# In the first down unit of a round P4 stands between P6 and P7, with a bank of its own, and the next norm's operands are made two products later

## The chip, the cores and the metric

The kernel runs on one core of a Trainium2 chip. The metric is the device time of one execution in microseconds (us): the median of three runs of the kernel before is 1251.46 us (1251.28 to 1251.55).

## The reference, cut to what matters

The program is one inference step of a two-layer decoder for 576 tokens (512 of a prompt, 64 of samples) and a model width of 1024. Each layer is a mixer and then an MLP; the change touches only the MLP's second product and the operands of the norm that follows it.

```python
def sqrelu_mlp(h, w_up, w_down):
    return jnp.square(jax.nn.relu(h @ w_up)) @ w_down
...
hp = hp + sqrelu_mlp(rmsnorm(hp, norm_mlp[l]), mlp_w_up[l], mlp_w_down[l])
```

`w_up` is 1024 x 4096, `w_down` is 4096 x 1024, everything in float32.

## The kernel before

**Operands in two parts.** TensorE (PE) multiplies a rounded type, so each float32 operand is cut into a high and a low part, and every product is three sets of matmuls: high weight by high activation, high weight by low activation, low weight by high activation. For a weight block of 128x512, ScalarE (ACT) makes the high part (`whi`, line 248) and VectorE (DVE) the low part (`wlo`, line 259). Six buffers of each exist (`NW_`). The raw weights come by DMA in tiles of 512 KB (`raw`, line 218), three buffers, in the order in which they are used.

**Rounds.** The 4096 inner columns of an MLP are done in four rounds of 1024. A round has eight up products (48 matmuls each), whose results are made into activations, and then a down part that adds into the residual `h0` to `h7` (128 rows of the model width by 576 tokens each). The last round of the second layer is done in another way, so seven rounds have the down part that the change touches: four in the first MLP (P6 of their unit 0 starts at 317.14, 417.22, 516.00 and 617.33 us of the span) and three in the second (895.57, 994.33 and 1093.17 us).

**Down units.** The down part of a round is four units, `m` = 0 to 3; unit `m` adds to rows `h[2m]` and `h[2m+1]`. A unit is a 2x2 block product done with seven products instead of eight (Winograd's form of Strassen's scheme): P1 to P7, each of 12 matmuls of 128x288. The weights of P1, P2 and P4 are blocks a11, a12 and a22 of the unit's two raw tiles; those of P5, P6, P7 and P3 are sums s1 to s4 that DVE makes first (line 233): s1 = a21+a22, s2 from s1 and a11, s3 from a21 and a11, s4 from s2 and a12. `UNIT` is the order of the products in units 1 to 3 (P1, P5, P6, P2, P7, P3, P4), `FIRST_UNIT` the order in unit 0.

**Chains through the banks.** Intermediate sums stay in PSUM: P6 is added onto P1 in bank `x` (half of an `acc` tile), ACT copies that to a bank `z`, P7 is added onto it there, ACT copies that to `w`, P4 is added there. DVE takes each finished bank into `h` (`to_h`, line 511). The banks `y`, `f`, `g`, `z`, `w` are four buffers in turn. In unit 0 the P1, P2, P3 and P5 products go first (three of their four parts while the last activations are still being made), P1's result is kept in `v`, the other half of the same `acc` tile, and then come P6, P7 and P4. In units 1 to 3, `y` is a copy of P1's bank, made between P1 and P6 (line 546), `z` one of P6's (line 552), `w` one of P7's (line 557).

**What sets the order.** DVE and ACT run in the order in which the code issues to them (`manual_schedule`); TensorE's order is left to a scheduler. After each product `ahead_to` issues the casts, low parts and sums for the weights of later products (up to five ahead), so those stand in the DVE and ACT queues between the `to_h` operations and the copies.

**Between two reads of one PSUM tile** by different engines the build puts a wait: in unit 0 the copy `z<-x` (line 535) stands behind DVE's `h += v` (the third call on line 511 after `shared(f)`), since `v` and `x` are one tile.

**The next norm.** In the fourth round of the first MLP each finished residual row goes to `nxt.chunk`: ACT makes `xhi` (line 391) and a square (line 401), DVE `xlo` (line 392), GpSimd (POOL) adds the square to a sum (line 407). Those calls stand right after the unit that finished the rows. They are the operands of the next layer's projections.

Of the kernel before, what the change touches and what calls it, by code (L numbers as in the profile page):

```python
# [14 lines left out]
ALU = mybir.AluOpType  # L15
# [98 lines left out]
NCOL = 59  # L114
UNIT = ("P1", "P5", "P6", "P2", "P7", "P3", "P4")
SUMS = {"P1": "s1", "P5": "s2", "P2": "s3", "P6": "s4"}
FIRST_UNIT = ("P1", "P2", "P3", "P5", "P6", "P7", "P4")


@with_exitstack  # L120
def hybrid_step(ctx: ExitStack, tc: tile.TileContext, a, o):
    nc = tc.nc
# [27 lines left out]
    h, first = [], []  # L150
# [37 lines left out]
    def add_unit(pair, first):  # L188
        jobs.extend((n, len(order)) for n in (FIRST_UNIT if first else UNIT))
        order.extend(pair)  # L190
# [17 lines left out]
    used, done, summed = [0], [0], [0]  # L208
# [17 lines left out]
    def total(k, i):  # L226

        if (k, i) not in sums:
            b = blocks_of(i)
            x, y = {"s1": ("a21", "a22"), "s2": ("s1", "a11"), "s3": ("a21", "a11"), "s4": ("s2", "a12")}[k]  # L230
            x = b[x] if x in b else total(x, i)
            sums[k, i] = sum_pool[0].tile([P, 512], F32, name=k, tag="sum", bufs=4)
            nc.vector.tensor_tensor(out=sums[k, i], in0=x, in1=b[y], op=ALU.add)  # L233
        return sums[k, i]
# [37 lines left out]
    def ahead_to(n):  # L272

        n = min(n, len(jobs))
        while len(parts) < n or owed:
            while summed[0] < min(len(parts) + 2, len(jobs)):
                job, i = jobs[summed[0]]
                k = SUMS.get(job)
                if k:
                    total(k, i)  # L280
                summed[0] += 1
            if len(parts) < n:
                prepare()
            split_low()
        load_to(done[0] + 3)
# [144 lines left out]
    def rounds_of(norm, nxt, mp):  # L430
        rounds = 32 // FB
# [12 lines left out]
        for r in range(rounds):  # L444
            plain = nxt is None and r == rounds - 1
            acts = []
# [36 lines left out]
                acts.append((hi, lo))  # L483
            if plain:
                return [acts[2 * p + j] for j in range(2) for p in range(FB // 2)]
            for m in range(KC // 2):
                down_unit(acts, m, m == 0)
                if r == rounds - 1:
                    nxt.chunk(2 * m)
                    nxt.chunk(2 * m + 1)  # L490

    def down_unit(acts, m, first):


        operand = {"P1": 0, "P2": 2, "P3": 1, "P5": 3, "P6": 4, "P7": 5, "P4": 6}
        row1, row2 = h[2 * m], h[2 * m + 1]
        both = acc_tile()
        x, v = both[:, 0, 0:TH], both[:, 1, 0:TH]
        n2, n1 = slice(0, TH), slice(TH, T)

        def bank(name):
            return m_tile(name)[:, 0:TH]

        def run(n, out, start, stop=True, ks_=range(4), w=None, ahead=NW_ - 1):
            w = w or take(1)[0]
            product(out, w, lambda k: [t[:, operand[n]] for t in acts[k]], ks_, start, stop)
            if ahead:
                ahead_to(used[0] + ahead)

        def to_h(row, cols_, src, op):  # L510
            nc.vector.tensor_tensor(out=row[:, cols_], in0=row[:, cols_], in1=src, op=op)  # L511

        def shared(src):
            to_h(row1, n2, src, ALU.add)
            to_h(row2, n2, src, ALU.subtract)

        if first:

            y, g, f = bank("y"), bank("g"), bank("f")
            early = [("P1", x), ("P2", y), ("P3", g), ("P5", f)]  # L520
            ws = take(4)
            for (n, out), w in zip(early, ws):
                run(n, out, True, False, range(3), w, 0)
            for (n, out), w in zip(early, ws):
                run(n, out, False, True, [3], w, 0)
                if n == "P1":
                    nc.scalar.copy(out=v, in_=x)
            ahead_to(used[0] + 2)
            run("P6", x, False, ahead=2)
            to_h(row1, n1, y, ALU.add)  # L530
            to_h(row1, n2, g, ALU.add)
            shared(f)
            to_h(row1, n1, v, ALU.add)
            z = bank("z")
            nc.scalar.copy(out=z, in_=x)
            to_h(row1, n2, x, ALU.add)
            run("P7", z, False, ahead=3)
            w_ = bank("w")
            nc.scalar.copy(out=w_, in_=z)
            to_h(row2, n2, z, ALU.subtract)  # L540
            run("P4", w_, False, ahead=4)
            to_h(row2, n1, w_, ALU.subtract)
            return
        run("P1", x, True)
        y = bank("y")
        nc.scalar.copy(out=y, in_=x)  # L546
        f = bank("f")
        run("P5", f, True)
        shared(f)
        run("P6", x, False)  # L550
        z = bank("z")
        nc.scalar.copy(out=z, in_=x)
        run("P2", y, False)
        to_h(row1, n1, y, ALU.add)
        run("P7", z, False)
        w_ = bank("w")
        nc.scalar.copy(out=w_, in_=z)
        to_h(row2, n2, z, ALU.subtract)
        run("P3", x, False)
        to_h(row1, n2, x, ALU.add)  # L560
        run("P4", w_, False)
        to_h(row2, n1, w_, ALU.subtract)
# [774 lines left out]
```

## Time and profile before

| | |
|---|---|
| median of three runs | 1251.46 us |
| the profiled execution | 1251.84 us |
| its span, first to last instruction | 1249.8 us |
| mean granted TensorE clock | 0.991 |
| PE busy | 1207.0 us, 97% |
| DVE busy | 850.8 us, 68% |
| ACT busy | 585.7 us, 47% |
| POOL busy | 193.2 us, 15% |

A row of the timeline has the start, the duration, the engine, the line, the operation with output and inputs, and, in brackets, how long the engine had been idle and what ended that. "x4" merges four instructions in a row; PE instructions overlap, so what four matmuls cost is read from one start to the next. A row of a table of windows has the stretch, its length, the engine's busy time and number of instructions, the mean granted TensorE clock (1.00 is full), the DMA share and GB/s.

### The profile page before, as it was taken

The numbers are of one execution on the slowest core, as the hardware profiler recorded it, in microseconds if no ns is written. First come the engines' busy times: TensorE is split into PE (matmuls) and PEld (weight loads), VectorE is DVE, ScalarE is ACT, GpSimd is POOL, SyncE is SP. The second block draws the span as 40 slices with busy tenths as digits, with TensorE's granted clock in tenths as the row PEclk, the third lists the DMA queues.
The fourth block names the chain that finished last, engine by engine and source line by source line (L and its number), as shares of the span: only waits on it lengthen the run. The fifth ranks groups of instructions, "written<-read, shape, count | busy, mean of one in ns | idle before, by whom it ended". The sixth has DMA issues, their size and how long they took to land.

```text
span 1249.8 us, 22699 instructions
## 1 busy us (share of the span) xinstructions
PE 1207.0 (97%) x9213; PEld 1190.4 (95%) x9213; DVE 850.8 (68%) x1539; ACT 585.7 (47%) x1108; POOL 193.2 (15%) x166
## 2 busy tenths in 40 slices
PE   8999999999999999999999999999999999999996
PEld 8999999999999999999989988999999999999996
DVE  8877785456856866775796778546875784784455
ACT  5333554444434434443466777444443453443363
POOL 3543330110000000000023554220000000000223
PEclk9999999999999999899999999999999999999998
DMA  7244222222232242142224212122132233124253
GB/s 278 95 128 122 72 87 72 81 68 85 69 119 68 68 119 85 51 121 69 65 85 123 69 35 69 52 85 68 52 122 80 68 101 103 51 86 118 84 150 113
DMA packets 38521, 113.62 MB, mean 91 GB/s; under 512 B 4161, under 2 KB 11521, under 8 KB 38401
## 3 DMA queue, kind: packets, MB, share of 16 engines
q1 hardware_dynamic: 37408, 110.31, 29.0%
q8 instruction: 72, 1.18, 0.4%
q0 software_dynamic: 320, 1.31, 0.3%
q10 hardware_dynamic: 688, 0.55, 0.1%
q14 instruction: 33, 0.26, 0.1%
HBM read 107.12 MB, written 6.03 MB: 91 GB/s over the span
## 4 chain that ended last, share of the span: by engine, by line
PE 87%; DVE 6%; ACT 3%; issue 2%; DMA 1%; SPq 0%; DVEq 0%; POOL 0%; ACTq 0%
PE acc L304 54%; PE acc L311 9%; PE dn L304 4%; PE z L311 4%; PE w L311 4%; PE y L311 3%; PE f L311 3%; DVE wlo L259 1%; DVE h L511 1%; ACT s L1023 1%; PE sp L1064 1%; PE op L1096 1%; PE g L311 1%; PE tpp L1083 1%; ACT whi L248 1%
## 5 line engine op out<-in xcount | busy, mean ns | idle before, releaser
L304 PE MATMUL acc<-xhi,whi 128*128 128x288 f32 x1520 | 328.5, 298 | 0.3 <-DVE vz L698 0.3
L304 PE MATMUL acc<-xhi,wlo 128*128 128x288 f32 x1520 | 325.7, 296 | 0.0
L304 PE MATMUL acc<-xlo,whi 128*128 128x288 f32 x1520 | 325.0, 295 | 0.0
L259 DVE TENSOR_TENSOR wlo<-raw,whi 128x512 fp32r<-128x512 f32 x340 | 247.6, 741 | 92.2 <-ACT whi L248 90.2
L248 ACT CAST whi<-raw 128x512 fp32r<-128x512 f32 x340 | 203.8, 617 | 151.8 <-PE acc L304 112.2
L304 PEld LDWEIGHTS acc<-xhi,whi 128*128 128x128 f32 x1520 | 244.0, 189 | 1.8 <-issue 1.3
L304 PEld LDWEIGHTS acc<-xhi,wlo 128*128 128x128 f32 x1520 | 245.0, 189 | 0.3
L304 PEld LDWEIGHTS acc<-xlo,whi 128*128 128x128 f32 x1520 | 244.6, 189 | 0.0
L462 ACT ACTIVATE q<-t 128x576 f32<-128x576 f32 x64 | 43.9, 686 | 241.8 <-DVE t L457 241.8
L407 POOL TENSOR_TENSOR ssq<-ssq,sq 128x576 f32<-128x576 f32 x25 | 37.9, 1516 | 516.3 <-ACT sq L401 516.0
L457 DVE SCALAR_TENSOR_TENSOR t<-acc,rstd 128x576 f32<-128x576 f32 x64 | 48.3, 754 | 95.9 <-PE acc L304 95.7
L259 DVE TENSOR_TENSOR wlo<-s,whi 128x512 fp32r<-128x512 f32 x112 | 78.8, 714 | 13.1 <-ACT whi L248 13.1
L248 ACT CAST whi<-s 128x512 fp32r<-128x512 f32 x112 | 66.9, 619 | 41.4 <-DVE s L233 32.4
L473 DVE TENSOR_TENSOR alo<-q,ahi 128x864 fp32r<-128x864 f32 (+1 forms) x56 | 67.5, 1205 | 7.2 <-ACT ahi L472 7.2
L472 ACT CAST ahi<-q 128x864 fp32r<-128x864 f32 (+1 forms) x56 | 58.2, 1039 | 11.9 <-DVE q L480 11.0
L465 POOL TENSOR_TENSOR alo<-q,ahi 128x576 fp32r<-128x576 f32 x8 | 11.4, 1429 | 335.7 <-ACT ahi L464 335.7
L311 PE MATMUL acc<-ahi,whi 128*128 128x288 f32 x308 | 56.3, 302 | 2.5 <-ACT y L546 2.5
L233 DVE TENSOR_TENSOR s<-raw 128x512 f32<-128x512 f32 x56 | 38.4, 686 | 29.8 <-DMA raw<-in_w_dn 29.8
L311 PE MATMUL acc<-ahi,wlo 128*128 128x288 f32 x308 | 54.7, 296 | 0.0
L311 PE MATMUL acc<-alo,whi 128*128 128x288 f32 x308 | 54.5, 295 | 0.0
L311 PEld LDWEIGHTS acc<-ahi,whi 128*128 128x128 f32 x308 | 46.9, 194 | 3.2 <-ACT y L546 3.2
L304 PE MATMUL acc<-olo,whi 128*128 128x288 f32 x208 | 46.4, 297 | 0.0
(324 smaller groups left out, 2159.6 us busy)
## 6 DMA issues: line engine op xcount, KB each, us to landing
raw<-in_w_dn SPq DMA_DIRECT2D x72, 512.0 KB
raw<-in_w_up SPq DMA_DIRECT2D x64, 512.0 KB
raw<-in_w_in SPq DMA_DIRECT2D x22, 512.0 KB
raw<-in_w_o SPq DMA_DIRECT2D x16, 512.0 KB
raw<-in_w_qkv SPq DMA_DIRECT2D x10, 512.0 KB
h<-in_xT SPq DMA_DIRECT2D x8, 288.0 KB
s<-in_s SPq DMA_DIRECT2D x4, 512.0 KB
out_ret_s<-s SPq DMA_DIRECT2D x4, 512.0 KB
```

The lines of the kernel that those rows point to most:

```text
L233: nc.vector.tensor_tensor(out=sums[k, i], in0=x, in1=b[y], op=ALU.add)
L248: nc.scalar.copy(out=hi, in_=src)
L259: nc.vector.tensor_tensor(out=lo, in0=src, in1=hi.bitcast(F32), op=ALU.subtract)
L304: nc.tensor.matmul(out, lhsT=w_, rhs=x_[:, hf if isinstance(hf, slice) else half(hf)], start=(start and si == 0), stop=(stop and si == 2))
L311: nc.tensor.matmul(out, lhsT=w[wi][:, k * P:(k + 1) * P], rhs=x(k)[xi], start=(start and k == ks_[0] and si == 0), stop=(stop and k == ks_ ...
L407: nc.gpsimd.tensor_tensor(out=self.ssq, in0=self.ssq, in1=sq, op=ALU.add)
L457: nc.vector.scalar_tensor_tensor(out=halves(t), in0=view, scalar=0.0, in1=norm.rv, op0=ALU.max, op1=ALU.mult)
L462: nc.scalar.activation(out=flat(q[:, seg]), in_=t, func=AF.Square)
L472: nc.scalar.copy(out=hi[:, s0 - 1:s1 - 1], in_=q[:, s0:s1])
L473: nc.vector.tensor_tensor(out=lo[:, s0 - 1:s1 - 1], in0=q[:, s0:s1], in1=hi.bitcast(F32)[:, s0 - 1:s1 - 1], op=ALU.subtract)
L511: nc.vector.tensor_tensor(out=row[:, cols_], in0=row[:, cols_], in1=src, op=op)
L1023: nc.scalar.activation(out=s[:, n, cut_:], in_=s[:, n, cut_:], func=AF.Exp, bias=nm[:, n:n + 1], accum_out=den[:, n:n + 1])
```

## The change

`FIRST_UNIT` becomes P1, P2, P3, P5, P6, P4, P7. In unit 0, P4 is a product of its own in bank `w` instead of being added onto the copy of P6 and P7, so the copy `w<-z` goes; DVE subtracts both `w` and `z` from `h[2m+1]`, one operation more. The reads of `y` and `g` come ahead of the weights for P4 and P7, the copy `z<-x` ahead of the read of `v`. In the fourth round of the first MLP, `nxt.chunk` for the rows of unit `m` is called inside unit `m+1`: the first after the copy of P6's bank, the second after the copy of P7's; those of the last unit stay behind it.

```diff
-FIRST_UNIT = ("P1", "P2", "P3", "P5", "P6", "P7", "P4")
+FIRST_UNIT = ("P1", "P2", "P3", "P5", "P6", "P4", "P7")
...
+            between = []
             for m in range(KC // 2):
-                down_unit(acts, m, m == 0)
-                if r == rounds - 1:
-                    nxt.chunk(2 * m)
-                    nxt.chunk(2 * m + 1)
+                down_unit(acts, m, m == 0, between, nxt)
+                between = [2 * m, 2 * m + 1] if r == rounds - 1 else []
+            for c in between:
+                nxt.chunk(c)
...
-            ahead_to(used[0] + 2)
-            run("P6", x, False, ahead=2)
             to_h(row1, n1, y, ALU.add)
             to_h(row1, n2, g, ALU.add)
+            ahead_to(used[0] + 2)
+            run("P6", x, False, ahead=0)
             shared(f)
-            to_h(row1, n1, v, ALU.add)
             z = bank("z")
             nc.scalar.copy(out=z, in_=x)
+            ahead_to(used[0] + 2)
+            to_h(row1, n1, v, ALU.add)
             to_h(row1, n2, x, ALU.add)
-            run("P7", z, False, ahead=3)
             w_ = bank("w")
-            nc.scalar.copy(out=w_, in_=z)
+            run("P4", w_, True, ahead=3)
+            to_h(row2, n1, w_, ALU.subtract)
+            run("P7", z, False, ahead=4)
+            to_h(row2, n1, z, ALU.subtract)
             to_h(row2, n2, z, ALU.subtract)
-            run("P4", w_, False, ahead=4)
-            to_h(row2, n1, w_, ALU.subtract)
...
         nc.scalar.copy(out=z, in_=x)
+        for c in between[0:1]:
+            nxt.chunk(c)
         run("P2", y, False)
...
         to_h(row2, n2, z, ALU.subtract)
+        for c in between[1:2]:
+            nxt.chunk(c)
         run("P3", x, False)
```

ACT's row in the first down unit of the first round before, from the copy to `v` to the first copy of unit 1. In brackets are the engines or DMA queues on which an instruction waits (the number behind the underscore has no meaning here). The sums are named by buffer: s_3508 is s3 of unit 0, s_3668, s_3696, s_3723 and s_3702 are s1, s2, s3 and s4 of unit 1.

```order
L527 COPY acc<-acc 128x288 [waits PE_49]
L248 CAST whi<-s_3508 128x512
L248 CAST whi<-raw 128x512 [waits DMAHW4_49]
L535 COPY z<-acc 128x288 [waits DVE_49]
L248 CAST whi<-raw 128x512 [waits DMAHW5_49]
L248 CAST whi<-s_3668 128x512
L539 COPY w<-z 128x288 [waits PE_49]
L248 CAST whi<-s_3696 128x512 [waits DVE_49]
L248 CAST whi<-raw 128x512
L248 CAST whi<-s_3723 128x512 [waits DVE_49,Activation_49]
L248 CAST whi<-s_3702 128x512 [waits PE_49,Activation_49]
L546 COPY y<-acc 128x288 [waits PE_49]
```

The same place of the changed kernel; s_3676, s_3697, s_3722 and s_3703 are now s1 to s4 of unit 1.

```order
L528 COPY acc<-acc 128x288 [waits PE_49]
L248 CAST whi<-raw 128x512 [waits DMAHW4_49]
L535 COPY z<-acc 128x288 [waits PE_49,Activation_49]
L248 CAST whi<-s_3508 128x512
L248 CAST whi<-raw 128x512 [waits DMAHW5_49]
L248 CAST whi<-s_3676 128x512 [waits DVE_49]
L248 CAST whi<-s_3697 128x512 [waits DVE_49]
L248 CAST whi<-raw 128x512
L248 CAST whi<-s_3722 128x512 [waits DVE_49,PE_49,Activation_49]
L248 CAST whi<-s_3703 128x512 [waits PE_49,Activation_49]
L548 COPY y<-acc 128x288 [waits PE_49]
```

The copy `z` waits for PE instead of DVE, P7's cast (s_3508) moved behind it, P4's cast ahead of it, and the copy `w` is gone; the copy `y` still stands behind the casts of s3 and s4 of unit 1.

DVE's row in the same place before, from the read of `v` to the sum s3 of unit 1.

```order
L511 TENSOR_TENSOR h_70<-h_70,acc 128x288 [waits PE_49]
L511 TENSOR_TENSOR h_70<-h_70,acc 128x288 [waits Activation_49]
L233 TENSOR_TENSOR s_3696<-s_3668,raw 128x512 [waits DMAHW5_49]
L259 TENSOR_TENSOR wlo<-raw,whi 128x512 [waits Activation_49]
L233 TENSOR_TENSOR s_3702<-s_3696,raw 128x512 [waits DVE_49]
L259 TENSOR_TENSOR wlo<-s_3668,whi 128x512 [waits Activation_49]
L511 TENSOR_TENSOR h_74<-h_74,z 128x288 [waits Activation_49]
L233 TENSOR_TENSOR s_3723<-raw 128x512
```

The changed kernel, from the sum s1 of unit 1 to its s3.

```order
L233 TENSOR_TENSOR s_3676<-raw 128x512 [waits DMAHW6_49]
L259 TENSOR_TENSOR wlo<-s_3508,whi 128x512 [waits Activation_49]
L512 TENSOR_TENSOR h_70<-h_70,acc 128x288
L512 TENSOR_TENSOR h_70<-h_70,acc 128x288 [waits DVE_49]
L233 TENSOR_TENSOR s_3697<-s_3676,raw 128x512 [waits DMAHW5_49,DVE_49]
L259 TENSOR_TENSOR wlo<-raw,whi 128x512 [waits Activation_49]
L233 TENSOR_TENSOR s_3703<-s_3697,raw 128x512 [waits DVE_49]
L259 TENSOR_TENSOR wlo<-s_3676,whi 128x512 [waits Activation_49]
L512 TENSOR_TENSOR h_74<-h_74,w 128x288 [waits PE_49]
L233 TENSOR_TENSOR s_3722<-raw 128x512
```

The low part of P7's weights (s_3508) moved to just ahead of the reads of `v` and `x`, and it waits for ACT; from there to s3 of unit 1 the two rows hold the same work.

ACT's row in unit 1 of the fourth round before, where the operands of the next norm stand; h_70 and h_74 are rows 0 and 1 of the residual, s_7008 and s_6987 are s3 and s4 of unit 1.

```order
L248 CAST whi<-raw 128x512
L391 ACTIVATE xhi<-h_70,cols 128x576
L401 ACTIVATE ssq<-h_70 128x576
L391 ACTIVATE xhi<-h_74,cols 128x576 [waits DVE_49]
L401 ACTIVATE sq<-h_74 128x576
L248 CAST whi<-s_7008 128x512 [waits Activation_49]
L248 CAST whi<-s_6987 128x512 [waits PE_49,Activation_49]
L546 COPY y<-acc 128x288 [waits PE_49]
```

The changed kernel, from the copy `y` of unit 1 on; s_7057 and s_7079 are s1 and s2 of unit 2.

```order
L548 COPY y<-acc 128x288 [waits PE_49]
L248 CAST whi<-raw 128x512 [waits DMAHW6_49,Activation_49]
L248 CAST whi<-raw 128x512 [waits DMAHW7_49,PE_49,Activation_49]
L554 COPY z<-acc 128x288 [waits PE_49]
L391 ACTIVATE xhi<-h_70,cols 128x576
L401 ACTIVATE ssq<-h_70 128x576
L248 CAST whi<-s_7057 128x512 [waits DVE_49,Activation_49]
L248 CAST whi<-s_7079 128x512 [waits DVE_49,PE_49,Activation_49]
L561 COPY w<-z 128x288 [waits PE_49]
L391 ACTIVATE xhi<-h_74,cols 128x576
L401 ACTIVATE sq<-h_74 128x576
```

The four operations on rows 0 and 1 moved from ahead of the copy `y` to behind the copies `z` and `w`.

More of the change, by code (lines that the diff above doesn't have):

```diff
@@ L485, in rounds_of, with down_unit @@
                 return [acts[2 * p + j] for j in range(2) for p in range(FB // 2)]
+            between = []
             for m in range(KC // 2):
-                down_unit(acts, m, m == 0)
-                if r == rounds - 1:
-                    nxt.chunk(2 * m)
-                    nxt.chunk(2 * m + 1)
-    def down_unit(acts, m, first):
+                down_unit(acts, m, m == 0, between, nxt)
+                between = [2 * m, 2 * m + 1] if r == rounds - 1 else []
+            for c in between:
+                nxt.chunk(c)
+    def down_unit(acts, m, first, between, nxt):
         operand = {"P1": 0, "P2": 2, "P3": 1, "P5": 3, "P6": 4, "P7": 5, "P4": 6}
```

## Prediction

> **What bounds the kernel now.** I read the page first, for the busiest engine, and then what that engine waits for.
>
> ```profile
> PE 1207.0 (97%) x9213; PEld 1190.4 (95%) x9213; DVE 850.8 (68%) x1539; ACT 585.7 (47%) x1108; POOL 193.2 (15%) x166
> PE z L311 <- ACT z L535: 18.1, 7, 2.6
> PE acc L311 <- ACT y L546: 2.5, 3, 1.3
> PE tpp L1083 <- ACT pT L1086: 2.4, 1, 2.4
> ```
>
> PE is the bound: 97% busy, and the waits that it has are few. The largest is in the edited unit: seven times, once in each round, 18.1 us in all, PE stands at P7 until ACT has copied `z`. The second largest is the copy `y` of units 1 to 3, three times, all in the fourth round. The third lies elsewhere.
>
> How much time hangs on the first wait shows in windows from the start of P6 in unit 0 to the start of P5 in unit 1. They hold four products, 48 matmuls, in each of the seven rounds; the eighth window is four products without a wait. Columns: stretch, length, PE busy and instructions, granted clock, DMA.
>
> ```profile
> 317.14:327.87 10.73, 8.14 (x50) 0.84 0.18 51
> 417.22:426.64 9.42, 6.84 (x50) 1.00 0.19 56
> 516.00:527.96 11.96, 9.38 (x50) 0.71 0.19 50
> 617.33:628.08 10.75, 8.17 (x50) 0.84 0.16 50
> 895.57:904.98 9.41, 6.83 (x51) 1.00 0.17 56
> 994.33:1003.74 9.41, 6.83 (x51) 1.00 0.18 57
> 1093.17:1102.58 9.41, 6.83 (x51) 1.00 0.21 57
> 426.64:432.99 6.35, 6.35 (x51) 1.00 0.29 90
> ```
>
> Four products cost 6.35 us, 1.59 each. The rounds lose 4.38, 3.07, 5.61, 4.40, 3.06, 3.06 and 3.06 us: 26.64. That is more than the 18.1 of idle time, because in three rounds the clock falls after the wait (0.84, 0.71, 0.84) and the next matmuls run slowly. Those rounds lose 1.3, 2.5 and 1.3 us more than the rest.
>
> The second wait the same way: seven products without a wait, and three windows of the fourth round with one copy `y` each (seven, seven and six products).
>
> ```profile
> 426.64:437.76 11.12, 11.12 (x86) 1.00 0.29 96
> 628.08:640.08 12.00, 11.40 (x86) 1.00 0.33 93
> 640.08:652.15 12.07, 11.42 (x86) 1.00 0.27 84
> 652.15:663.22 11.07, 9.80 (x75) 1.00 0.46 141
> ```
>
> Against 11.12, 11.12 and 9.53 (six of 1.59) these lose 0.88, 0.95 and 1.54: 3.37 us. So at most 26.64 + 3.37 = 30.0 us can be won.
>
> Why does P7 wait so long? In the second round, whose clock is full, PE, then ACT, then DVE:
>
> ```profile
> 418.29 0.69 PE L311 MATMUL acc<-ahi,wlo 128*128 128x288 f32 x4
> 421.56 0.79 PE L311 MATMUL z<-ahi,whi 128*128 128x288 f32 x4 [2.58 <-ACT z L535]
> 429.27 0.69 PE L311 MATMUL acc<-ahi,wlo 128*128 128x288 f32 x4
> 434.58 0.69 PE L311 MATMUL w<-ahi,whi 128*128 128x288 f32 x4
> ```
>
> ```profile
> 421.12 0.38 ACT L535 COPY z<-acc 128x288 f32<-128x288 f32 x1 [3.46 <-DVE h L511]
> 421.42 0.62 ACT L248 CAST whi<-raw 128x512 fp32r<-128x512 f32 x1
> 425.45 1.14 ACT L248 CAST whi<-s 128x512 fp32r<-128x512 f32 x2 [0.56 <-DVE s L233]
> 426.84 0.38 ACT L546 COPY y<-acc 128x288 f32<-128x288 f32 x1 [0.25 <-PE acc L311]
> 430.00 0.38 ACT L552 COPY z<-acc 128x288 f32<-128x288 f32 x1 [1.45 <-PE acc L311]
> 433.64 0.39 ACT L557 COPY w<-z 128x288 f32<-128x288 f32 x1
> ```
>
> ```profile
> 420.64 0.45 DVE L511 TENSOR_TENSOR h<-h,acc 128x288 f32<-128x288 f32 x1
> 421.54 0.46 DVE L511 TENSOR_TENSOR h<-h,acc 128x288 f32<-128x288 f32 x1 [0.45 <-ACT z L535]
> 421.91 0.68 DVE L233 TENSOR_TENSOR s<-s,raw 128x512 f32<-128x512 f32 x1
> 422.51 0.69 DVE L259 TENSOR_TENSOR wlo<-raw,whi 128x512 fp32r<-128x512 f32 x1
> 424.68 0.68 DVE L233 TENSOR_TENSOR s<-raw 128x512 f32<-128x512 f32 x1
> 425.89 0.68 DVE L259 TENSOR_TENSOR wlo<-raw,whi 128x512 fp32r<-128x512 f32 x1
> 430.38 0.69 DVE L233 TENSOR_TENSOR s<-raw 128x512 f32<-128x512 f32 x1 [2.24 <-DMA raw<-in_w_dn]
> 441.02 0.69 DVE L233 TENSOR_TENSOR s<-raw 128x512 f32<-128x512 f32 x1 [1.75 <-DMA raw<-in_w_dn]
> ```
>
> P6 ends at 418.98, but the copy starts only at 421.12, behind DVE's read of `v` (420.64 + 0.45). In unit 1 the same kind of copy starts 0.04 us after its product (429.96 to 430.00).
>
> **The change part by part.** *P4 between P6 and P7.* I count from the start of P6 (417.22 above). P6 ends at 1.76; P4 needs no copy, and its high weights are cast before P6's copy, so PE goes on. The copy `z` starts at 1.80 and ends at 2.18, while P7 is due only at 2 x 1.59 = 3.18. P7's cast follows the copy by 0.30 (421.12 to 421.42), so it runs 2.10 to 2.72, in time as well; its low part, cast end + 0.03 and 0.69 long, is ready by 3.44, needed from 3.18 + 1.06. So the old wait goes, with the slow clock behind it. The copy `w` that goes and the `h` operation that comes (0.45 us a round) lie on ACT and DVE beside PE.
>
> *What is late next.* The same DVE queue still makes the weights of unit 1 and 2, and PE now comes 3.07 us sooner. First the copy `y` of unit 1: ACT holds it behind the casts of s3 and s4. DVE: P7's low part at 2.75, 0.60 to the next (421.91 to 422.51), two reads of 0.37 each, so s2 at 4.09; from s2 to s3 the queue is what it was, 2.77 (421.91 to 424.68), so s3 runs 6.86 to 7.54. Then 0.09 to ACT (425.36 to 425.45), two casts of 0.52 step, so the copy runs 8.67 to 9.05. PE wants P6 of unit 1 after five products, at 7.94: a wait of about 1.1 us, where before there was none.
>
> Second, the raw tile of unit 2. It goes into the buffer that the low part of a12 (425.89) sets free; that operation is 1.21 behind s3, so it ends at 8.75 instead of 9.35. From its end to the sum that waits for the tile are 3.81 us (426.57 to 430.38): s1 of unit 2 starts at 12.56. From there to the end of the copy `w` of unit 1 it was 3.65 (430.38 to 434.03), so P4 of unit 1 can start at 16.2 or a little later; nine products put it at 14.3. So 1.92 us are lost in all by then, the 1.1 at the copy `y` included. It is the same sum seen as slack: before, PE reached P4 0.55 us after its copy; the chain comes 0.60 sooner, PE 3.07. A wait makes the first four matmuls a tenth slower:
>
> ```profile
> 655.17 0.80 PE L311 MATMUL acc<-ahi,whi 128*128 128x288 f32 x4 [1.27 <-ACT y L546]
> 655.81 0.68 PE L311 MATMUL acc<-alo,whi 128*128 128x288 f32 x4
> ```
>
> That is 0.64 between starts instead of 0.53. I take 1.92 + 0.11 = 2.03 us a round. After that no chain falls behind: DVE and DMA together take 10.64 us a unit (from 430.38 to 441.02, the same sum of the next unit, which waits for its tile too), PE 11.12.
>
> Six rounds then go from 22.24 lost (26.64 - 4.40) to 6 x 2.03 = 12.2: 10.0 us won.
>
> *The fourth round.* Here the moved operands of the next norm take the copy `y` out from behind two casts, two squares and what they wait for. That alone would give 3.37, and with unit 0 up to 4.40 + 3.37 = 7.77. But DVE is nearly full in this round; its window from the last activation to the end of the last `xlo`, that operation, and the PE row that needs it:
>
> ```profile
> 616.75:668.51 51.76, 48.37 (x77) 0.97 0.34 101
> 667.70 0.81 DVE L392 SCALAR_TENSOR_TENSOR xlo<-h,cols,xhi 128x576 fp32r<-128x576 f32 x1
> 669.08 0.42 PE L304 MATMUL acc<-xlo,whi 128*128 128x288 f32 x2
> ```
>
> DVE is idle for 3.39 us there and gets 0.45 more to do, so its last operation can come at most 2.9 us sooner; PE has 0.57 us of slack to it. At most 3.5 us of the 7.77 can be won unless POOL's adds slow DVE less at their new places; DVE will keep some waits. I take 3.0, the row's bound, and keep 1 and 5 for the range.
>
> Sum: 10.0 + 3.0 = 13.0. The profiled execution took 1251.84, so 1238.8; the median of the runs lies 0.38 lower: **1238.4 us**.
>
> A rule of the Trainium skill against a row. The rows say that a wait of 2.58 us dropped the clock in three of seven rounds, and that 1.27 us did not. The skill's page "TensorE: Matmul & The Clock Gate" (section "The HAM clock gate") has the clock halved after an idle window of about 3.4 us. By that the 2.58 would never drop it, and an estimate would leave the 5.1 us of slow clock to another cause that stays; the time would then be 1243.5. The rows decide: the three slow stretches start right at the wait.
>
> **The rivals.** *A: the waits are mostly absorbed.* The order of the queues may leave DVE more ahead, or tiles land sooner. For: DVE is idle 2.24 us for the tile at 430.38, so any earlier release helps at once. Against: the 3.81 us are in the trace, and the DVE chain is counted from rows of the same round. If half of the 12.2 went, and the fourth round gave 4: 1238.4 - 6.1 - 1 = 1231.
>
> *B: more is given back.* A tile that lands 0.7 us later in each round, or units 2 and 3 waiting too (DVE's margin is 11.12 - 10.64 = 0.5 us a unit), costs 7 x 0.7 = 5: 1243.4. With a whole microsecond more it is 1246.
>
> *C: slower, the clock.* The round now has two short waits (1.1 and 0.8 us) instead of a long one. If the pair drops the clock as the long one did in the third round (5.61 - 3.07 = 2.54), each round pays 2.54 more: 7 x 2.54 = 17.8, 1238.4 + 17.8 = 1256.2. It decides from six such drops on (13.0 / 2.54 = 5.1). Against it: three waits of 0.60, 0.65 and 1.27 us in the fourth round stood in windows of full clock (1.00 above). The same skill page ("A second HAM failure mode: psum-queue depth-cycling") says that short idles between groups of matmuls, often enough, make the clock swing; that would be this case, and no row here shows it.
>
> *D: nothing is won.* If every microsecond that PE is early is waited for in front of the weights, the time stays at 1251. The 0.60 us that the chain gains a round and the fallen clock speak against it: a chain that moves with `z` cannot lose all of 30 us.
>
> **How the numbers follow.** The forecast (1234 to 1242) gets 0.58, A (1226 to 1234) 0.16, B (1242 to 1247) 0.15, C 0.05, D 0.06. The range is 1230 to 1245, which leaves out C, D and the ends of A and B, about 0.2. A measurement of this kernel can tell about 0.2% (2.5 us) from no change. Faster by more than that: 0.58 + 0.16 + 0.15 = 0.89; within it 0.06, slower 0.05.
>
> **What would show it right or wrong.** Right: no wait of PE on the copy `z` in unit 0; a wait of about 1 us at P6 of unit 1 on the copy `y` and one of 0.5 to 0.9 at P4 of unit 1 on the copy `w`, in all seven rounds; the window from P6 of unit 0 to P5 of unit 1 at 6.35 us, P6 of unit 1 about 9.05 us behind P6 of unit 0; granted clock 1.00 there. In the fourth round no wait on `y` in units 2 and 3, and DVE busy almost without a gap to its last `xlo`. Wrong: a clock below 1.00 after the short waits (C), no PE wait in unit 1 (A), or waits in units 2 and 3 of the other rounds (B).

## The result and the profile after

| | before | after |
|---|---|---|
| median | 1251.37 us (4 runs, 1249.74 to 1251.55) | 1242.06 us (4 runs, 1241.18 to 1244.38) |
| the profiled execution | 1251.84 us, span 1249.8 | 1244.38 us, span 1242.3 |
| mean granted clock in it | 0.991 | 0.993 |

The ratio is 0.9931, with a 95% interval of 0.9914 to 0.9949: faster by 0.5 to 0.9%. The forecast was 1238.4 with a range of 1230 to 1245. The profiled execution of after is the slowest of its four.

The page of after still has PE at 97%:

```profile
PE 1205.8 (97%) x9213; PEld 1187.3 (96%) x9213; DVE 852.9 (69%) x1546; ACT 581.2 (47%) x1101; POOL 192.2 (15%) x166
```

Its waits of PE, the largest first (us in all, times, longest):

```profile
PE acc L311 <- ACT y L548: 7.8, 7, 1.1
PE w L311 <- ACT w L561: 4.5, 8, 2.0
PE acc L304 <- DVE xlo L392: 2.7, 2, 2.4
...
PE tpp L1089 <- ACT pT L1092: 2.4, 1, 2.4
```

The 18.1 us on the copy `z` are gone. In their place stand seven waits on the copy `y` and eight on the copy `w`, one of each in every round and one more on `w` of 2.0; and a wait on `xlo` of 2.4, which before did not have.

The stretch from P6 of unit 0 to P5 of unit 1 in rounds 1, 4, 5 and 7 of after (PE alone: length, busy, instructions, clock, DMA):

```profile
317.52:323.89 6.37, 6.37 (x50) 1.00 0.30 85
...
610.47:616.83 6.36, 6.36 (x51) 1.00 0.30 85
891.24:897.60 6.36, 6.36 (x51) 1.00 0.28 82
...
1086.77:1093.13 6.36, 6.36 (x51) 1.00 0.28 82
```

PE runs through at full clock. The starts also give the length of the rounds, against those of the same windows of before:

| from P6 of unit 0 of round | before | after | won |
|---|---|---|---|
| 1 to 4 | 300.19 | 292.95 | 7.24 |
| 4 to 5, with the norm and the second mixer between | 278.24 | 280.77 | -2.53 |
| 5 to 7 | 197.60 | 195.53 | 2.07 |

So the ordinary rounds won what the forecast gave them, and the stretch from the fourth round to the fifth lost.

An ordinary round (the second) of after: PE, ACT, DVE.

```profile
424.40 0.79 PE L311 MATMUL acc<-ahi,whi 128*128 128x288 f32 x4 [1.12 <-ACT y L548]
431.32 0.80 PE L311 MATMUL w<-ahi,whi 128*128 128x288 f32 x4 [0.29 <-ACT w L561]
```

```profile
422.91 1.14 ACT L248 CAST whi<-s 128x512 fp32r<-128x512 f32 x2 [1.71 <-DVE s L233]
423.95 0.39 ACT L548 COPY y<-acc 128x288 f32<-128x288 f32 x1
...
430.34 0.62 ACT L248 CAST whi<-s 128x512 fp32r<-128x512 f32 x1 [1.33 <-DVE s L233]
430.87 0.39 ACT L561 COPY w<-z 128x288 f32<-128x288 f32 x1
```

```profile
422.12 0.68 DVE L233 TENSOR_TENSOR s<-raw 128x512 f32<-128x512 f32 x1
...
427.61 0.69 DVE L233 TENSOR_TENSOR s<-raw 128x512 f32<-128x512 f32 x1 [1.68 <-DMA raw<-in_w_dn]
```

P6 of unit 0 starts at 415.21. The copy `y` follows two casts without a gap, and those waited 1.71 us for s3, whose sum starts at 422.12. P1's result had been ready since about 421.7 (its last four matmuls start at 421.01, 0.69 long). The copy `w` follows a cast in the same way.

The fourth round: from the first product of unit 0 to the first matmul of the V projection, and the 8 us behind that, before (first fence) and after (second).

```profile
610.94:670.15 59.21, 54.10 (x391) 0.97 0.32 94
670.15:678.15 8.00, 8.00 (x62) 1.00 0.32 95
```

```profile
604.11:663.65 59.54, 53.37 (x391) 0.99 0.33 97
663.65:671.65 8.00, 8.00 (x54) 0.85 0.24 66
```

It took 59.54 instead of 59.21, and then the clock is at 0.85: 54 matmuls instead of 62 in 8 us, 1 us more. PE, DVE and POOL in that round of after:

```profile
640.06 0.79 PE L311 MATMUL w<-ahi,whi 128*128 128x288 f32 x4 [2.04 <-ACT w L561]
653.05 0.42 PE L304 MATMUL acc<-xhi,whi 128*128 128x288 f32 x2
661.49 0.54 PE L304 MATMUL acc<-xlo,whi 128*128 128x288 f32 x2 [2.42 <-DVE xlo L392]
```

```profile
622.79 0.69 DVE L233 TENSOR_TENSOR s<-raw 128x512 f32<-128x512 f32 x1 [1.60 <-DMA raw<-in_w_dn]
...
635.79 1.25 DVE L233 TENSOR_TENSOR s<-raw 128x512 f32<-128x512 f32 x1 [1.77 <-DMA raw<-in_w_dn]
...
657.54 1.43 DVE L958 TENSOR_SCALAR bq<-cols 128x8 f32<-128x8 f32 x1
...
659.49 1.95 DVE L392 SCALAR_TENSOR_TENSOR xlo<-h,cols,xhi 128x576 fp32r<-128x576 f32 x1
```

```profile
657.45 3.37 POOL L407 TENSOR_TENSOR ssq<-ssq,sq 128x576 f32<-128x576 f32 x2 [4.14 <-ACT sq L401]
```

PE ends the down units 48.94 us after the round's start (604.11 to 653.05, the first row of a projection that needs every `xhi` and `xlo`); before it was 52.28 (610.94 to 663.22). But the last `xlo` ends at 57.33, where before it ended at 57.57. From 635.79, when the last tile of the round lets it go on, DVE has no gap until that `xlo` is done at 661.44: 25.65 us. Some of its operations there take twice as long as elsewhere and more (`xlo` usually 0.81), and each of those lies beside one of POOL's adds.

### The profile page after: what moved, and what is told of

The parts are those of the page before. It is cut to its first block, busy times and chain, and to the rows that moved or that the text cites. A ratio compares the mean times of both kernels' runs of the same rounds, so it can differ in the third digit from the quotient of the medians.

```text
span 1242.3 us, 22717 instructions
## 1 busy us (share of the span) xinstructions
PE 1205.8 (97%) x9213; PEld 1187.3 (96%) x9213; DVE 852.9 (69%) x1546; ACT 581.2 (47%) x1101; POOL 192.2 (15%) x166
## 4 chain that ended last, share of the span: by engine, by line
PE 82%; DVE 10%; ACT 3%; issue 3%; DMA 2%; SPq 0%; DVEq 0%; POOL 0%; ACTq 0%
PE acc L304 54%; PE acc L311 7%; PE dn L304 4%; DVE wlo L259 3%; PE y L311 3%; PE w L311 2%; PE f L311 2%; PE z L311 2%; DMA raw<-in_w_dn 1%; DVE s L233 1%; DVE h L512 1%; DVE xlo L392 1%; PE g L311 1%; PE tpp L1089 1%; ACT whi L248 1%
## 5 line engine op out<-in xcount | busy, mean ns | idle before, releaser
L259 DVE TENSOR_TENSOR wlo<-raw,whi 128x512 fp32r<-128x512 f32 x340 | 250.3, 749 | 90.0 <-ACT whi L248 88.1
L259 DVE TENSOR_TENSOR wlo<-s,whi 128x512 fp32r<-128x512 f32 x112 | 75.6, 685 | 13.5 <-ACT whi L248 13.5
L233 DVE TENSOR_TENSOR s<-raw 128x512 f32<-128x512 f32 x56 | 40.9, 730 | 32.0 <-DMA raw<-in_w_dn 32.0
L304 PE MATMUL acc<-ohi,wlo 128*128 128x288 f32 x208 | 46.4, 296 | 0.0
```

The lines of the kernel that those rows point to most:

```text
L259: nc.vector.tensor_tensor(out=lo, in0=src, in1=hi.bitcast(F32), op=ALU.subtract)
L304: nc.tensor.matmul(out, lhsT=w_, rhs=x_[:, hf if isinstance(hf, slice) else half(hf)], start=(start and si == 0), stop=(stop and si == 2))
```

## The experiments

The theories as they stand in the expectations below: T1, ACT's order makes the new waits, since copies stand behind casts that wait for DVE; T3, the weights are late in any case; T4, the product between P6 and P7 is what took the old wait away; T2, moving the norm's operands is harmful in itself; T5, POOL's adds slow DVE and so make the end of the fourth round late; T6, it is the length of DVE's queue. Others are told where they come. Each ratio is to runs of before taken beside that experiment; where two experiments are compared by their medians, their intervals say how far that carries.

### The copies ahead of the casts

```diff
-        run("P1", x, True)
+        run("P1", x, True, ahead=0)
         y = bank("y")
         nc.scalar.copy(out=y, in_=x)
+        ahead_to(used[0] + NW_ - 1)
...
-        run("P7", z, False)
+        run("P7", z, False, ahead=0)
         w_ = bank("w")
         nc.scalar.copy(out=w_, in_=z)
+        ahead_to(used[0] + NW_ - 1)
```

> After, with the copies y and w of units 1 to 3 issued ahead of the casts of the weights that follow the product, not behind them. T1 (PE waits for the copies because they stand behind casts in ACT's order): the waits on y at P6 and on w at P4 of unit 1 go, and the casts that now stand behind the copies are still in time, by a microsecond or more. Each of the seven rounds wins its 2.0 us of waits: 1242 - 6 x 2.0 = 1230, and 1 to 2 more in the fourth round, about 1228. T3 (the sums of DVE and the tiles are late anyway, whichever stands first on ACT): PE waits the same time one or two products later, in front of weights or low parts; 1240 to 1242.

Measured: 1231.09 us (4 runs), ratio to before 0.9836 [0.9813, 0.9858]. Its largest waits in the down units and behind them:

```profile
PE acc L304 <- DVE xlo L392: 2.6, 2, 2.3
...
PE acc L311 <- ACT y L548: 1.2, 2, 0.6
```

The waits on `w` are gone, and those on `y` are left in the fourth round only, twice. The copy `z` of unit 0 shows the round's length, here and in after:

```profile
414.82 0.38 ACT L535 COPY z<-acc 128x288 f32<-128x288 f32 x1 [1.92 <-PE acc L311]
510.66 0.38 ACT L535 COPY z<-acc 128x288 f32<-128x288 f32 x1 [1.92 <-PE acc L311]
```

```profile
417.05 0.38 ACT L535 COPY z<-acc 128x288 f32<-128x288 f32 x1 [1.92 <-PE acc L311]
514.68 0.38 ACT L535 COPY z<-acc 128x288 f32<-128x288 f32 x1 [1.92 <-PE acc L311]
```

95.84 against 97.63: 1.8 us a round. T1 holds and T3 falls: PE waits for no weight in the ordinary rounds, so only the copies were late. Six rounds of 1.8 make 10.8 of the 11.0 us between the medians (1242.06 to 1231.09); the 1 to 2 us expected of the fourth round did not come, since its wait on `xlo` (2.3) stayed.

### Each half of the first unit's edit

The product between was taken out (P7 behind P6 again, P4 last, the rest as in after):

```diff
-            run("P4", w_, True, ahead=3)
-            to_h(row2, n1, w_, ALU.subtract)
-            run("P7", z, False, ahead=4)
+            run("P7", z, False, ahead=3)
             to_h(row2, n1, z, ALU.subtract)
             to_h(row2, n2, z, ALU.subtract)
+            run("P4", w_, True, ahead=4)
+            to_h(row2, n1, w_, ALU.subtract)
```

> After, with P7 right behind P6 again and P4 last; the bank of its own, the copy ahead of the read of v and of P7's cast, and all the rest stay. T1 (the wait on z was long because the copy stood behind DVE's read of v and the rest of the queue): PE waits for the copy alone, 0.4 to 0.7 us at P7 instead of 2.6, and part of that comes off the wait on y in unit 1, which is set by DVE: 0 to 0.7 us a round more than after, 1242 to 1247. T4 (the product between is what does it): the wait on z is 2 us or more again, and the time is 1249 or more.

And the other way round, the product between with the order of issue of before:

```diff
+            ahead_to(used[0] + 2)
+            run("P6", x, False, ahead=2)
             to_h(row1, n1, y, ALU.add)
             to_h(row1, n2, g, ALU.add)
-            ahead_to(used[0] + 2)
-            run("P6", x, False, ahead=0)
             shared(f)
+            to_h(row1, n1, v, ALU.add)
             z = bank("z")
             nc.scalar.copy(out=z, in_=x)
-            ahead_to(used[0] + 2)
-            to_h(row1, n1, v, ALU.add)
```

> After, with the product between and the bank of its own, but the copy z, the casts and the reads of unit 0 issued in the order of before: the copy behind DVE's read of v and behind two casts. T1 (the order on ACT and DVE decides): the copy z ends some 4.3 us after P6's start and P7 wants it at 3.2, so PE waits 0.4 to 1.1 us there, P4's low part is later too, and the wait on y in unit 1 is shorter by most of that; a round is 0.3 to 1 us longer than in after, 1244 to 1249. T4 (the product between is what does it): as after, 1241 to 1243.

Measured: 1246.17 us (10 runs), ratio 0.9958 [0.9942, 0.9973], and 1246.91 us (7 runs), 0.9968 [0.9951, 0.9985]. The second round's waits, of the first kernel and of the second:

```profile
417.57 0.80 PE L311 MATMUL z<-ahi,whi 128*128 128x288 f32 x4 [0.53 <-ACT z L535]
...
424.84 0.40 PE L311 MATMUL acc<-ahi,whi 128*128 128x288 f32 x1 [0.67 <-ACT y L548]
...
431.82 0.79 PE L311 MATMUL w<-ahi,whi 128*128 128x288 f32 x4 [0.34 <-ACT w L561]
```

```profile
419.03 0.76 PE L311 MATMUL w<-ahi,whi 128*128 128x288 f32 x4 [0.61 <-DVE h L512]
421.00 0.79 PE L311 MATMUL z<-ahi,whi 128*128 128x288 f32 x4 [0.16 <-ACT z L536]
426.42 0.79 PE L311 MATMUL acc<-ahi,whi 128*128 128x288 f32 x4 [0.40 <-ACT y L547]
```

Without the product between, the wait on `z` is 0.53 instead of 2.58: the order of issue takes four fifths of it away without that product, against T4. Part of what is saved there comes back at `y` (0.67) and at `w` (0.34). With the old order the product between does nearly as much: the wait on `z` is 0.16, not the 0.4 to 1.1 foreseen, with 0.61 at P4, whose bank DVE still reads. From the second round's copy `z` to the third's it is 98.07 and 98.28 us in these two kernels, 97.63 in after and 98.77 in before. Either half alone ends 4 to 5 us above after in the medians, as T1 had it; both are needed for the last of it. The profiled execution of the first kernel is the fastest of its ten (1242.75), that of the second the second slowest of its seven (1249.06). P4's bank of its own stays in both kernels and was not tested alone.

### The norm's operands: each part of the change alone

The first unit of after, `nxt.chunk` called as in before:

```diff
             for m in range(KC // 2):
-                down_unit(acts, m, m == 0, between, nxt)
-                between = [2 * m, 2 * m + 1] if r == rounds - 1 else []
-            for c in between:
-                nxt.chunk(c)
+                down_unit(acts, m, m == 0, [], nxt)
+                if r == rounds - 1:
+                    nxt.chunk(2 * m)
+                    nxt.chunk(2 * m + 1)
```

> The first unit of after, but in the fourth round the operands of the next norm come where before had them, right after each unit. T1 (ACT's order decides): the six other rounds win 10 us over before, as in after. In the fourth round ACT then has two scaled casts and two squares of the norm, with their waits on DVE, ahead of the copy y of unit 1, while PE is 3 us earlier: PE waits about 4 us there in one piece, the wins of unit 0 are given back there, and the waits on y in units 2 and 3 stay at 1.0 to 1.6 us. Fourth round within 2 us of before, so 1240 to 1244 in all, no faster than after, more by the clock if the 4 us drop it. T2 (the move of the norm's operands is what spoilt the fourth round, where after lost 2.5 us to before): without it the fourth round wins about 3 instead of losing 2.5, and the time is about 1237.

Measured: 1240.76 us (5 runs), ratio 0.9917 [0.9896, 0.9937], so no slower than after, as T1 had it. The wait in unit 1 of the fourth round, and the two windows of that round:

```profile
622.77 1.33 PE L311 MATMUL acc<-ahi,whi 128*128 128x288 f32 x4 [4.21 <-ACT y L547]
```

```profile
604.13:664.19 60.06, 54.43 (x390) 0.94 0.31 93
664.19:672.19 8.00, 8.00 (x62) 1.00 0.31 94
```

PE stands 4.21 us in one piece, and its next matmuls take 1.33 instead of 0.79; yet the V projection starts 60.06 us after the round's start, only 0.52 later than in after, and then at full clock. What the moved operands win in the units is waited for at the end. Of the waits on `y` that T1 left in units 2 and 3 only unit 3's is there (1.42).

The other part alone, the first unit of before with the operands moved (the lines of the first unit go back to those of before, among them):

```diff
-FIRST_UNIT = ("P1", "P2", "P3", "P5", "P6", "P4", "P7")
+FIRST_UNIT = ("P1", "P2", "P3", "P5", "P6", "P7", "P4")
...
-            run("P4", w_, True, ahead=3)
+            run("P7", z, False, ahead=3)
+            w_ = bank("w")
+            nc.scalar.copy(out=w_, in_=z)
...
+            run("P4", w_, False, ahead=4)
```

> The first unit of before, with the operands of the next norm two products later, as in after. T1: the waits of PE on the copy z in unit 0 stay in all seven rounds, 2.6 us each, so six rounds are as in before. In the fourth round the three waits on y go (3.37 us), but DVE's queue, with little idle time, gives the last low part of the norm no sooner: at most 1 to 2 us are won, 1249.5 to 1251. T2 (the move is harmful by itself): the fourth round loses some 2 to 5 us and the time is 1253 to 1256.

Measured: 1254.61 us (12 runs), ratio 1.0025 [1.0008, 1.0042], slower. Its fourth round ends with the same wait:

```profile
666.48 0.53 PE L304 MATMUL acc<-xlo,whi 128*128 128x288 f32 x2 [2.41 <-DVE xlo L392]
```

T1 expected a small gain here and was wrong; T2's figure came out. But T2 as a rule does not hold: with both cures below, the kernel with the move is the faster one in the medians.

### POOL's adds

The adds of squares of chunks 1 to 7 are left out in the fourth round, so that norm divides by the first chunk's squares alone.

```diff
-        def chunk(self, c):
+        def chunk(self, c, add=True):
             self.operands(c)
-            self.square(c)
+            self.square(c, add=add or c == 0)
...
-                nxt.chunk(c)
+                nxt.chunk(c, False)
```

> After, with POOL's seven adds of squares in the fourth round left out (the sum of squares of that norm is then that of its first chunk alone). T5 (the adds slow the operations of DVE that run beside them, and so make the end of DVE's queue late): the last xlo takes 0.81 instead of 1.95, bq 0.1 instead of 1.43, s and wlo 0.69 instead of 1.5 to 1.8; PE's waits on xlo (2.42), sql (0.34) and on w in unit 2 (2.04, to about 1) shrink, and the slow clock behind them (1.5) goes: about 5 us, 1237. T6 (the length of DVE's queue, not the adds, makes the end late): 1241 to 1243, and the wait on xlo is 2 us or more.

Measured: 1235.98 us (6 runs), ratio 0.9878 [0.9854, 0.9902]. PE's only wait in units 2 and 3, and DVE's rows as shown of after:

```profile
638.67 0.79 PE L311 MATMUL w<-ahi,whi 128*128 128x288 f32 x4 [0.76 <-ACT w L561]
```

```profile
634.96 0.69 DVE L233 TENSOR_TENSOR s<-raw 128x512 f32<-128x512 f32 x1 [1.81 <-DMA raw<-in_w_dn]
...
653.40 0.16 DVE L958 TENSOR_SCALAR bq<-cols 128x8 f32<-128x8 f32 x1
...
654.07 0.81 DVE L392 SCALAR_TENSOR_TENSOR xlo<-h,cols,xhi 128x576 fp32r<-128x576 f32 x1
```

From the sum of the last tile to the end of the last `xlo` it is 19.92 us (634.96 to 654.88), where after took 25.65: the same queue of operations, 5.73 us shorter. That is what the adds cost there, more than the wait at the end. The adds cost the kernel before about as much (below, in the part on the fourth round). The tile came 1.0 us sooner as well (30.67 us from the round's start at 604.29, where after had 31.68). T5 holds, T6 falls.

One add of after from close by, DVE and POOL:

```profile
627.87 0.45 DVE L512 TENSOR_TENSOR h<-h,y 128x288 f32<-128x288 f32 x1
628.24 1.56 DVE L233 TENSOR_TENSOR s<-raw 128x512 f32<-128x512 f32 x1
```

```profile
627.80 1.44 POOL L407 TENSOR_TENSOR ssq<-ssq,sq 128x576 f32<-128x576 f32 x1 [363.35 <-ACT sq L401]
```

The sum, whose two inputs lie in SBUF, ends 0.56 us after the add does (629.80 and 629.24) and takes 1.56 instead of 0.69; the addition into `h`, which reads a PSUM bank, began inside the same add and took its usual 0.45. The Trainium skill's page "SBUF — State Buffer" (section "SBUF: two separate sides") says that a GpSimd operation and a VectorE operation with two SBUF inputs need the same pair of ports, and that the later one is blocked for the whole of the other. The trace agrees.

### The end of DVE's queue, and both cures together

Three operations are taken out ahead of the last two `xlo`: `bq8` is made by POOL at the start of the kernel, and the V projection's weights are prepared behind the norm's operands.

```diff
+    nc.gpsimd.tensor_scalar(out=bq8, in0=cols[:, COL["b_qkv"]:COL["b_qkv"] + KC], scalar1=SCALE_S, scalar2=None,
+                            op0=ALU.mult)
...
             for c in between:
                 nxt.chunk(c)
+            if r == rounds - 1:
+                ahead_to(used[0] + 4)
...
-        run("P7", z, False)
+        run("P7", z, False, ahead=4 if end else 5)
...
-        run("P3", x, False)
+        run("P3", x, False, ahead=3 if end else 5)
...
-        run("P4", w_, False)
+        run("P4", w_, False, ahead=2 if end else 5)
```

`end` is true in unit 3 of the fourth round.

> After, with three operations of DVE taken out ahead of the last two xlo of the fourth round: the scaling of bq is done by POOL at the kernel's start, and the low parts of the V chunk's weights are made behind the operands of the norm. T5 and T1 (PE waits at the end of the fourth round for a backlog of DVE): 1.43 + 0.6 + 0.6 = 2.6 us fewer stand before the last xlo, PE's wait there (2.42) goes to less than 0.5, the clock stays at 1.00, and 0.3 to 1 us may be waited for sql: 3 to 4 us won, about 1238.5. T7 (the end is set by the sum of squares on POOL or by xhi on ACT): PE waits about 2 us for sql in front of ms instead, the clock falls, and at most 1 us is won, 1241 to 1242.

Measured on after: 1239.6 us (6 runs), ratio 0.9906 [0.9883, 0.9929]. The wait on `xlo` at the end is gone; smaller ones stand at the norm's mean instead (0.30 and this one), and the clock stays at 1.00 there:

```profile
661.62 0.40 PE L374 MATMUL ms<-sql,ones_dr 128*128 128x288 f32 x1 [0.72 <-DVE sql L216]
```

That is T5's side of the expectation, with 2.5 us won in the median of the 3.5 expected; the interval overlaps that of after (0.9914 to 0.9949), so the trace shows this gain better than the time does. Then the same edit on the kernel with the copies first:

> The copies ahead of the casts (as in the run with the copies first, 1231.1) and the three operations out of the way of the last xlo. If the two losses of after are separate, the sum: 1231.1 - 3.5 = 1227.6. If the end of the fourth round is set elsewhere: 1230 to 1231.

Measured: 1225.88 us (5 runs), ratio 0.9802 [0.9778, 0.9827], the fastest kernel of this study: the two losses of after add up (16.2 us below after in the medians, 11.0 and 2.5 singly). Its fourth round, to the V projection:

```profile
599.29:655.62 56.33, 53.27 (x390) 1.00 0.28 85
```

And the same with the norm's operands where before had them (the edit is the loop shown above):

> As the run with both cures, but the operands of the next norm right after each unit, as in before. T1 (ACT's order decides): the copy y of unit 1 stands behind two scaled casts and two squares again, which wait for DVE's h; PE waits 2 to 4 us there in the fourth round and some 0.5 to 1.5 in units 2 and 3, but is then later at the end and waits for nothing there: 1 to 4 us slower than the run with both cures, 1229 to 1231. T2 (to move the norm's operands is harmful in itself): faster than the run with both cures by 1 us or more.

Measured: 1230.09 us (5 runs), ratio 0.9829 [0.9806, 0.9852]. PE waits 3.18 us for `y` in unit 1 of the fourth round and 1.19 in unit 3. With both cures the move is worth 4 us in the medians, though the two intervals overlap a little (0.9778 to 0.9827 with it, 0.9806 to 0.9852 without).

Last, the final two adds of squares on DVE instead of POOL:

```diff
-                nc.gpsimd.tensor_tensor(out=self.ssq, in0=self.ssq, in1=sq, op=ALU.add)
+                (nc.vector if late else nc.gpsimd).tensor_tensor(out=self.ssq, in0=self.ssq, in1=sq, op=ALU.add)
```

> The run with both cures, with the last two adds of squares of the fourth round on DVE instead of POOL. T5 (an add on POOL costs DVE about as much as it would take there, and is slower itself): the last xlo goes from 1.5 to 0.8, the two adds cost DVE 1.5, the sum of squares is ready 1 us sooner, PE's waits of 1.0 us at ms go or shrink to 0.3, about 1 us won: 1224.9. T8 (DVE is the bound at the end, so more work there is a loss): a wait on xlo or sql of 1 us or more, 1226 to 1227.

Measured: 1226.59 us (4 runs), ratio 0.9806 [0.9788, 0.9824]. In the trace the fourth round is 0.84 us shorter (55.49 to the V projection), the wait at the mean 0.19; in the time it can't be told from the kernel with both cures. Inconclusive.

## Why the forecast was right, and where a term was wrong

**The wait that goes.** Right. The copy `z` starts 1.84 us after P6's start (forecast 1.80), nothing of PE waits for it, and the windows are 6.36 us long (6.35) at full clock.

**What is late next.** Right in mechanism and size, for all seven rounds. Counted from P6 in the second round: s3 6.91 (forecast 6.86), copy `y` 8.74 (8.67), P6 of unit 1 9.19 (9.05), the sum of unit 2 that waits for its tile 12.40 (12.56), P4 of unit 1 16.11 (16.2). The waits are 1.12 and 0.29 us; the second is 0.26 to 0.44 in the seven rounds, shorter than the 0.5 to 0.9 foreseen. The six ordinary rounds were to win 10.0 us; the spans give 7.24 + 2.07 and, from round 7 to the end, 1.10 (156.63 to 155.53 us): 10.4. About 3.8 of it is the clock of rounds 1 and 3, which fell behind the wait on `z` in the profile of before. The forecast took it from the same profile; which rounds it hits changes from execution to execution (last section), so this part of the agreement is partly luck. A round without it, the second, went from 98.77 us (421.12 to 519.89 in before's copies `z`) to 97.63: 1.14 won, where the forecast gave 1.04 (3.07 - 2.03).

**The fourth round.** Wrong: 3.0 us were to be won, 0.33 were lost up to the V projection and 2.17 from there to P6 of round 5 (225.42 us before, 227.59 after). Of the latter 1.01 us comes before the second mixer's first long wait, with the slow clock behind the new wait on `xlo`; 1.16 comes behind it, where after has one more stretch of half clock than before (782.02 to 785.43 us of the span). The failing step is the one that read DVE's idle time of 3.39 us as time that its last operation can come sooner. It came 0.11 us sooner. The row of after for the same stretch of DVE:

```profile
609.85:661.50 51.65, 47.67 (x79) 1.00 0.36 104
```

There are still 3.98 us idle, and 3.37 of it is new: DVE waits 1.60 and 1.77 us for the tiles of units 2 and 3 (the second is the row at 635.79). The idle time of before did not wait for tiles, and when that went, the tiles stood behind it. The forecast had taken DVE and DMA together as 10.64 us a unit, less than PE's 11.12, from a unit without the norm's operands. With two `xlo` and an add beside it, the two sums that wait for tiles are 13.00 us apart (622.79 to 635.79), and 12.17 without the adds (622.79 to 634.96 in that kernel): here the tiles come more slowly than PE uses them. A tile comes only after DVE has made a low part from the one before it in its buffer, so a DVE with more to do gets its tiles later too. No run takes the tile waits away, so what they cost alone is not shown.

The adds, which the forecast named ("unless POOL's adds slow DVE less at their new places"), are no new cost. Summed over the operations of DVE that took longer than usual beside them, they cost 7.2 us in before and 6.7 in after. Two rows of before; such a low part usually takes 0.68:

```profile
642.53 1.92 DVE L259 TENSOR_TENSOR wlo<-s,whi 128x512 fp32r<-128x512 f32 x1
```

```profile
640.53 3.37 POOL L407 TENSOR_TENSOR ssq<-ssq,sq 128x576 f32<-128x576 f32 x2 [9.92 <-ACT sq L401]
```

So to leave them out wins much (6.1 us in the medians), but they are not what after lost against before. The lost 3.37 us of waits on `y` did go in part (in units 2 and 3 there is none), but PE then waits 2.04 for `w` in unit 2 and 2.42 for `xlo` at the end.

**The total.** From the fourth round to the fifth it came out at -2.5 us, outside the 1 to 5 that the range kept for the fourth. The time stayed in the range because the bounds kept for the rivals left room: the median (1242.06) is 2.9 us inside the upper end, the profiled execution (1244.38) 0.6. That much is luck.

**The clock.** Rival C (the short waits drop it) did not come: it is 1.00 behind every wait of 1.1 us in after. But it fell behind the new 2.42, and twice in the second mixer, once more than in before, which the forecast had not in its sum.

**The other rivals.** A (the waits are absorbed) did not come by itself, but the kernel with the copies first shows that they can be, by ACT's order at two places. B priced late tiles or waits in units 2 and 3 in all rounds; PE waited there in the fourth alone. D (nothing is won) is out.

## What to carry to other kernels

When a wait is taken away, look in the same in-order queue for the next operation that another engine needs, and ask what it stands behind; here two copies of 0.39 us behind casts that they don't depend on cost 1.8 us a round, and a change of order at two places got it back. Idle time of an engine is not slack until one knows what it waits for: a new wait, here for tiles that this engine itself releases, may stand right behind the old one. A chain that fits in an ordinary unit need not fit in one with more work: add that work to the chain before calling it short enough. An add on an idle engine is not free when it holds up a busy one.

## What the runs showed of the hardware

**The clock after a wait.** Over the twelve profiles, rounds and second mixer together, waits of PE of 1.0 to 1.5 us were never followed by a lower granted clock (31 waits). Of four waits of 2.0 to 2.1 us one was (the kernel without the product between, clock 0.69 in the next 3 us); of the 2.3 to 2.6 us long ones 17 of 30; of 3.18 and 4.21 us both. The same wait at the same place went both ways: P7's in before three times in seven. The second mixer's wait (2.41 us in the profile of after, granted clock 0.73 in the 3 us behind it) stands in the profile of every kernel here and dropped the clock in six of twelve. It did so in the profiled execution of after, whose mean clock is 0.993; another run of after with 0.996 took 1241.52.

The traces show more than a chance. In every trace with more than one half-clock stretch their starts lie whole multiples of 3.413 us apart (in before 321.76, 519.73, 622.13 and 721.12: 58, 30 and 29 steps), and each stretch is 3.41 or 6.83 us long, the one at the kernel's end aside. So the clock is judged in windows of that length on a fixed grid. PE in one such window of the third and one of the second round of before, which share out the same wait of 2.58 us differently:

```profile
516.32:519.73 3.41, 1.43 (x11) 1.00 0.25 43
417.33:420.74 3.41, 1.65 (x13) 1.00 0.24 32
```

The first has 1.98 us without work and the clock is halved from its end; the second has 1.76, and the clock stays. Over the twelve profiles (from 60 us on) all 19 full-clock windows with 1.89 us or more of PE waiting were followed by half clock, and of the 68 with 1.0 to 1.81 us one was (1.61). Waiting is not all that counts: in the second mixer of five profiles (after among them, at 782.02) the clock fell behind a row of narrow matmuls (128x64) in a window with 0.05 us of waiting at most. The Trainium skill's page "TensorE: Matmul & The Clock Gate" (section "The HAM clock gate") has the default clock return after an idle window of about 3.4 us that runs freely; the grid fits a window that runs freely, the length does not: 1.9 us inside one window were enough.

So a wait of 2.3 to 2.6 us costs its length and, more often than not, 1 to 2.5 us more, and the times of a kernel that has seven of them spread: on the chip of the first experiments before took 1247.3 us in an execution with a mean clock of 0.996 and 1257.9 in one with 0.986 (21 runs); the kernel with the copies first, with two such waits, 1229.8 to 1233.3 (4 runs).

**POOL beside DVE.** Seven adds of 1.4 to 1.8 us made operations of DVE 6.7 us longer in the fourth round of after (the sums of what each takes over its usual time), about 0.96 for each add. All of the slowed ones read SBUF alone, however small: a scaling of 128x8 that takes 0.16 alone took 1.43.
